# A hybrid decoder block: weights of the last two output jobs kept unsplit in scratch, and some loads moved to ScalarE's queue

## The chip, the core and the metric

The kernel runs on one core of a Trainium2 chip. The metric is device time in microseconds (us), the median of several runs. A profile of one further execution shows what each engine did: TensorE (PE, with its weight loads as PEld), VectorE (DVE), ScalarE (ACT), GpSimd (POOL) and SyncE (SP), which here issues most DMAs.

## The reference

One decoder block on a sequence of 2048 positions, width 1024, in float32. A normalised and modulated input is projected by `w_in` (1024 x 8192). One branch is a convolution, a gated linear recurrence and a product with `w_out_rnn`; the other is attention in three dilated windows and a product with `w_out_attn`. Both are merged by sigmoid gates and go through `w_o`:

```python
    y_rnn = (hr * jax.nn.silu(z_rnn.astype(jnp.float32))).astype(dt) @ w_out_rnn[l]
    ...
    y_attn = (o * jax.nn.silu(z_attn.astype(jnp.float32))).astype(dt) @ w_out_attn[l]
    merged = jax.nn.sigmoid(g_r + bg_r) * y_rnn + jax.nn.sigmoid(g_a + bg_a) * y_attn
    x = x + gate[:, None, :] * (merged @ w_o[l])
return rms_norm(x, g_final)
```

Each of `w_out_rnn`, `w_out_attn` and `w_o` is 1024 x 1024.

## The kernel before

**Split operands.** TensorE multiplies in float32r, a shortened float32. Each operand is therefore split into a high part, a copy made by ACT (`hi_act`, L157), and a low part, the operand less its high part, made by POOL (`lo_pool`, L163) or DVE (`lo_dve`, L166). A product is three matmuls (`mm3`, L149): high x high, high x low, low x high.

**Stage one, to about 1372 us.** The input projection is computed by a seven-product scheme (Strassen's) on 512-wide blocks: per product four steps of `mm3`. Its split operands go once to a scratch tensor `sD` and are loaded again, seven tiles ahead. Between these products, from 812 to 1282 us, `output_weights` prepares the two output projections: every five products it takes one of 32 pieces of 512 x 128, first the 16 of `w_out_rnn` (i = 0), then the 16 of `w_out_attn` (i = 1). It loads the piece into a tile `R` one product after its start, splits it after four (ACT, then POOL) and stores high and low part after six, from ACT's queue, into `wD[i, m, half]`. There each partition's high and low values lie side by side, 4 KB in a row.

**Stage two, to about 1960 us.** Attention, head by head. Between its pieces runs a generator, `steps`, that computes the two output projections as eight jobs: four blocks of 512 positions for the recurrence (weights i = 0, results into `mrT`), then four for attention (i = 1, results into `meT`). A job has eight tiles (m) of 128 output channels, a tile has eight steps (k), and a step is one `mm3` of 128 x 128 weights with 128 x 512 inputs `yh`, `yl`. Two weight tiles serve one output tile, four steps each:

- `load_w` at steps 1 and 5 issues, on SP, the load of the weight tile that is needed three half-tiles later (`load_wd`, L339, 512 KB from `wD`), into one of four buffers S0 to S3; it waits until TensorE is done with the buffer's last content.
- `load_g` at step 3 loads, on SP, this tile's gates and for attention also the recurrence's part: `fg<-gaT`, `fg<-mrT` (L1695, 256 KB each), from a pool of four buffers.
- `evict` at step 1 of the following tile multiplies PSUM by the gate (L1700, DVE) and adds the recurrence's part (L1702, DVE). There are two PSUM tiles.
- `store` at step 7 of the following tile stores the result from SP (L1707, `meT<-fg`).
- `load_y` and `split_y` fetch the next job's inputs (`R<-oT`, L345) and split them.

**Stage three, about 1960 to 2074 us.** The last 128 steps, which are the last two jobs (attention, blocks 2 and 3), run after attention has ended. A hand-written table fires further work after each step s = 0 to 127: `load_rows(k)` for k = 0 to 3 loads two 128 x 1024 pieces of `w_o` (L1827, on SP) at the start and at s = 16, 44 and 75; `build_rows(s, k)`, from s = 8, 32, 72 and 96, multiplies them by the gate (L1830, POOL, `gate_rows`) and forms sums and split parts B11 to T4 of the next stage (L1842 on DVE for the sums, then ACT with DVE or POOL); `load_left(0)` at s = 104 loads the first 1 MB of `meT` in two DMAs (L1879, SP).

**Stage four, to the end.** The product with `w_o`, again by seven products, the residual and the last normalisation.

Inside stages two and three the order on each engine is the order in which the code was written; buffers of a pool are assigned when the program is built. Every DMA of SP and ACT uses one of eight completion counters in turn, so it also waits for the DMA eight before it to have landed.

Of the kernel before, what the change touches and what calls it, by code (L numbers as in the profile page):

```python
# [10 lines left out]
F32 = mybir.dt.float32  # L11
F32R = mybir.dt.float32r
# [8 lines left out]
P = 128  # L21
S = 2048
D = 1024
KT = D // P
NB = 4
# [64 lines left out]
def decoder_block(ctx, tc, x, c, positions, g_norm, w_mod, b_mod, w_in, b_gate, conv_w, conv_b,  # L90
# [4 lines left out]
    def T(pool, shape, dt, tag, **kw):  # L95
        cnt[0] += 1
        return pool.tile(shape, dt, tag=tag, name=f"{tag}_{cnt[0]}", **kw)
# [3 lines left out]
    def scratch(name, shape):  # L101
        return nc.dram_tensor(name, shape, F32, kind="Internal").ap()
# [16 lines left out]
    sD = scratch("sD", [28 * 7, P, 2, KH, P])  # L119

    wD = scratch("wD", [2, KT, 2, P, 2, KH, P])

    cp = ctx.enter_context(tc.tile_pool(name="cp", bufs=1))
    class Pools:
# [31 lines left out]
    def hi_act(o, i):  # L156
        nc.scalar.activation(o, i, AF.Copy)  # L157
# [177 lines left out]
    def load_wd(i, m, half):  # L335
        x = n_w[0]
        n_w[0] += 1
        W[x] = t = T(pS, [P, 2, KH, P], F32R, f"S{x % 4}")
        nc.sync.dma_start(t[:].bitcast(F32), wD[i, m, half])  # L339
# [80 lines left out]
    def output_weights():  # L420

        parts = [(i, w, m, half) for i, w in enumerate((w_out_rnn, w_out_attn)) for m in range(KT) for half in range(2)]
        for x, (i, w, m, half) in enumerate(parts):
            v = {}

            def load(v=v, w=w, m=m, half=half):
                v["raw"] = raw_tile([P, KH, P])
                rows = slice(half * KH * P, (half + 1) * KH * P)
                nc.sync.dma_start(v["raw"][:], w[0, rows, m * P : (m + 1) * P].rearrange("(k p) m -> p k m", p=P))

            def split(v=v):
                v["h"] = T(wq, [P, KH, P], F32R, "s1", bufs=1)
                v["l"] = T(wq, [P, KH, P], F32R, "s2", bufs=1)
                hi_act(v["h"][:], v["raw"][:])
                lo_pool(v["l"][:], v["raw"][:], v["h"][:])

            def store(v=v, i=i, m=m, half=half):
                for l, n in enumerate("hl"):
                    nc.scalar.dma_start(wD[i, m, half, :, l], v[n][:].bitcast(F32))

            for d, fn in ((1, load), (4, split), (6, store)):
                after_prod.setdefault(n_prod[0] + 5 * x + d, []).append(fn)

    def total(dst, ps, u, perm=lambda ap: ap):
# [1202 lines left out]
            at(e + 2, TAIL, self.store)  # L1647

    stored = set()


    def steps(jobs):

        tiles = [(j, m) for j in range(len(jobs)) for m in range(KT)]
        Y, G = {}, {}

        def load_w(x):

            if x < 2 * len(tiles):
                assert x == n_w[0]  # L1660
                j, m = tiles[x // 2]
                load_wd(jobs[j][0], m, x % 2)

        def load_y(j, k):
            if j < len(jobs):
                w, ys, n = jobs[j]
                if ys is oT and (n, k) == (2, KT - 1):

                    Y0[False, n, k] = last_head[0].zt[:, 0].rearrange("p r j -> p (r j)")
                    return  # L1670
                if ys is oT and n == 2 and k >= KH:

                    t = T(ap_, [P, KQW], F32, "kraw", bufs=4)
                    nc.sync.dma_start(t[:, :CH], ys[k * P : (k + 1) * P, n * CH : (n + 1) * CH])
                    Y0[False, n, k] = t[:, :CH]
                    return
                assert ys is yaT or (n // 2, k, n % 2) in stored
                load_yd(ys, n, k)

        def split_y(j, k):  # L1680
            if j < len(jobs):
                Y[j, k] = yh, yl = [T(fl, [P, CH], F32R, tag, bufs=NY) for tag in ("yh", "yl")]
                w, ys, n = jobs[j]
                t = Y0.pop((ys is yaT, n, k))
                hi_act(yh[:], t[:])
                (lo_dve if k % 2 else lo_pool)(yl[:], t[:], yh[:])

        def load_g(t):
            j, m = tiles[t]
            w, ys, n = jobs[j]  # L1690
            at_ = slice(m * P, (m + 1) * P), slice(n * CH, (n + 1) * CH)
            G[t] = []
            for src in (grT,) if ys is yaT else (gaT, mrT):
                g = T(fl, [P, CH], F32, "fg", bufs=4)
                nc.sync.dma_start(g[:], src[at_])  # L1695
                G[t].append(g)

        def evict(t, ps):
            g = G[t]
            nc.vector.tensor_tensor(g[0][:], ps[:], g[0][:], ALU.mult)  # L1700
            if len(g) > 1:
                nc.vector.tensor_tensor(g[0][:], g[0][:], g[1][:], ALU.add)  # L1702

        def store(t):
            j, m = tiles[t]
            w, ys, n = jobs[j]
            nc.sync.dma_start((mrT if ys is yaT else meT)[m * P : (m + 1) * P, n * CH : (n + 1) * CH], G.pop(t)[0][:])  # L1707

        for k in range(KT):
            split_y(0, k)  # L1710
        yield
        last = None
        for t, (j, m) in enumerate(tiles):
            ps = T(pj, [P, CH], F32, "pj")
            for k in range(KT):
                if k % KH == 1:

                    load_w(2 * t + k // KH + 3)
                if k == 1 and t:
                    evict(t - 1, last)  # L1720
                if k == 3:
                    load_g(t)
                if k == 7 and t:
                    store(t - 1)
                wt = W[2 * t + k // KH]
                yh, yl = Y[j, k]
                mm3(ps[:], wt[:, 0, k % KH, :], wt[:, 1, k % KH, :], yh[:], yl[:], first=k == 0, last=k == KT - 1)
                if k % KH == KH - 1:
                    W.pop(2 * t + k // KH)


                x = m * KT + k - KT * (KT - 1)
                j1 = j + 1
                if m == 0:
                    x, j1 = x + KT * KT, j

                if j1 == NB + 2:

                    if -14 <= x < KT - 14:
                        load_y(j1, x + 14)  # L1740
                elif j1 and x in LOAD_Y:
                    load_y(j1, LOAD_Y[x])
                if j1 and x in SPLIT_Y:
                    split_y(j1, SPLIT_Y[x])
                yield
            last = ps
        evict(len(tiles) - 1, last)
        store(len(tiles) - 1)
# [75 lines left out]
    def load_rows(k):  # L1824
        for i in range(2):
            v[k, i] = t = stage(1 + i + 2 * (k % 2), [P, D])
            nc.sync.dma_start(t[:], w_o[0, (k + i * KH) * P : (k + i * KH + 1) * P, :])  # L1827

    def gate_rows(k, i):
        nc.gpsimd.tensor_tensor(v[k, i][:], v[k, i][:], v["gate"][:], ALU.mult)  # L1830
# [44 lines left out]
    def load_left(p):  # L1875
        for half in range(2):
            shape = [P, KH, 2 * P]
            A[p, half] = t = T(up[0], shape, F32, f"A{half}", bufs=2) if p else stage(1 + half, shape)
            nc.sync.dma_start(t[:], meT[half * KH * P : (half + 1) * KH * P, p * 2 * P : (p + 1) * 2 * P]  # L1879
                              .rearrange("(k p) j -> p k j", p=P))  # L1880

    def left(p, name):
# [161 lines left out]
    with tc.manual_schedule():  # L2044
        v["gate"] = stage(0, [P, D])
        nc.sync.dma_start(v["gate"][:], gateD[0:1, :].broadcast_to([P, D]))
        load_rows(0)
        for k in range(KH):
            build_rows((8, 32, 72, 96)[k], k)
            if k:  # L2050
                on((16, 44, 75)[k - 1], load_rows, k)
        on(LAST - 24, load_left, 0)
        early = {}
        for p in range(NP):
            for d, fn, args in left_events(p):
                x = 7 * p + d - 4
                if p or d > 2:
                    on_p(max(x, 1), fn, *args)
                else:
                    on(LAST - 12 + 4 * (d + 1), fn, *args)  # L2060
            if p:
                on_p(max(7 * p - 12, 0), load_left, p)
            if p > 1:
                on_p(7 * p - 2, load_rows_x, p)
        for s in range(LAST):
            next(fill)
            fire(s)
        next(fill, None)
        fire(LAST)
        assert not pend  # L2070
        pools.close("fl", "pR")
        up.append(pools.open("up", side="right", bufs=1))
        v["gf"] = T(up[0], [P, D], F32, "gf")
        load_rows_x(0)
        load_rows_x(1)
        nc.sync.dma_start(v["gf"][:], g_final.unsqueeze(0).broadcast_to([P, D]))
        fire_p()
        for p in range(NP):
            output_pair(p)
        assert not after  # L2080
# [30 lines left out]
```

## Time and profile before

| | us |
|---|---|
| median of 3 runs (2241.41 to 2246.01) | 2245.79 |
| the profiled execution | 2239.79 |
| its span, from first to last instruction | 2238.0 |

| engine | busy us | share of the span |
|---|---|---|
| PE | 2171.1 | 97% |
| PEld | 1834.1 | 82% |
| DVE | 1403.2 | 63% |
| ACT | 1267.8 | 57% |
| POOL | 1054.7 | 47% |

Over the whole span the DMA engines moved 580.99 MB, 260 GB/s. Matmuls overlap, so a busy share of PE is not its rate; the distance between the starts of matmuls is. In a row of the profile stand the source line, the engine, the operation, what it writes and reads, the count, the busy time and mean duration, and, after the bar, how long the engine was idle before it and what ended that.

### The profile page before, as it was taken

The page shows a single profiled execution, that of the slowest core. Times are in us where ns is not written, and L with a number is a line of the kernel's source. Part 1 is how long each engine was busy: PE and PEld are TensorE (multiplying, and loading weights), DVE is VectorE, ACT ScalarE, POOL GpSimd, SP SyncE. Part 2 cuts the span into 40 slices and gives each one's busy share as a digit, 9 for nine tenths or more (in the row PEclk, how much of TensorE's full clock was granted, in tenths as well). Part 3 has the DMA queues.
Part 4 walks back from the last instruction along what each step waited for, and adds up shares of the span by engine and source line. Part 5 has one row for each costly group of instructions (what it writes and reads, how often), then busy time and mean ns, then how long its engine had stood idle before and what let it go on. Part 6 is the DMA issues. An engine that isn't in the chain of part 4 may idle for free. (4 is left out here: it accounts for less than half of the span.)

```text
span 2238.0 us, 33996 instructions
## 1 busy us (share of the span) xinstructions
PE 2171.1 (97%) x11326; PEld 1834.1 (82%) x11326; DVE 1403.2 (63%) x2452; ACT 1267.8 (57%) x2524; POOL 1054.7 (47%) x784
## 2 busy tenths in 40 slices
PE   8999999999999999999999999999999998988998
PEld 5998888888778998888788887888888887866786
DVE  5838887878456815444445342566677777645787
ACT  6638678667543627556546302676778877522333
POOL 2457777767557422222222112455566666344443
PEclk9999999999999999999999999999999999999999
DMA  8367887887998368888888988987888886899543
GB/s 286 118 210 260 286 297 269 293 283 263 319 278 295 113 231 272 284 288 282 275 286 283 343 290 287 288 269 246 267 261 265 243 266 218 253 331 321 196 161 113
DMA packets 409827, 580.99 MB, mean 260 GB/s; under 512 B 72150, under 2 KB 270002, under 8 KB 408628
## 3 DMA queue, kind: packets, MB, share of 16 engines
q1 hardware_dynamic: 371668, 458.81, 64.5%
q10 hardware_dynamic: 37792, 119.97, 14.0%
q8 instruction: 90, 1.47, 0.3%
q14 instruction: 85, 0.70, 0.1%
q0 software_dynamic: 192, 0.05, 0.0%
HBM read 364.78 MB, written 213.91 MB: 259 GB/s over the span
## 5 line engine op out<-in xcount | busy, mean ns | idle before, releaser
L149 PE MATMUL pj<-yh,S 128*128 128x512 f32 x1024 | 372.3, 408 | 21.8 <-DMA S<-wD 10.6
L163 POOL TENSOR_TENSOR S<-R,S 128x512 fp32r<-128x512 f32 x168 | 256.0, 1532 | 173.1 <-ACT S L157 70.4
L149 PE MATMUL X<-T,S 128*128 128x512 f32 x1344 | 324.4, 390 | 4.4 <-ACT u L383 3.3
L149 PE MATMUL V<-T,S 128*128 128x512 f32 x1344 | 324.6, 390 | 3.6 <-DVE t L450 3.3
L149 PEld LDWEIGHTS X<-T,S 128*128 128x128 f32 x1344 | 251.3, 188 | 59.4 <-ACT u L383 5.0
L149 PEld LDWEIGHTS V<-T,S 128*128 128x128 f32 x1344 | 251.8, 188 | 58.3 <-DVE t L450 3.2
L149 PEld LDWEIGHTS pj<-yh,S 128*128 128x128 f32 x1024 | 195.6, 191 | 64.2 <-ACT yh L157 8.6
L149 PE MATMUL pj<-yl,S 128*128 128x512 f32 x512 | 204.5, 399 | 7.5 <-POOL yl L163 5.9
L163 POOL TENSOR_TENSOR S<-s,S 128x512 fp32r<-128x512 f32 x92 | 139.7, 1519 | 116.5 <-ACT S L157 73.0
L1417 ACT ACTIVATE pp<-pp,st 128x256 f32<-128x256 f32 (+3 forms) x256 | 133.8, 524 | 93.3 <-DVE st L1416 92.1
L149 PE MATMUL Z<-T,S 128*128 128x512 f32 x672 | 161.9, 390 | 0.0
L149 PE MATMUL Y<-T,S 128*128 128x512 f32 x672 | 161.8, 390 | 0.0
L149 PE MATMUL W<-T,S 128*128 128x512 f32 x672 | 161.6, 389 | 0.0
L149 PEld LDWEIGHTS W<-T,S 128*128 128x128 f32 x672 | 126.0, 188 | 27.0 <-issue 0.9
L149 PEld LDWEIGHTS Y<-T,S 128*128 128x128 f32 x672 | 125.9, 188 | 26.0
L149 PEld LDWEIGHTS Z<-T,S 128*128 128x128 f32 x672 | 125.8, 188 | 26.1
L166 DVE TENSOR_TENSOR ptl<-pT,pth 128x384 fp32r<-128x384 f32 (+1 forms) x160 | 97.8, 628 | 75.4 <-ACT pth L157 73.2
L163 POOL TENSOR_TENSOR s<-R,s 128x512 fp32r<-128x512 f32 x32 | 45.2, 1413 | 206.4 <-ACT s L157 189.2
L157 ACT ACTIVATE S<-R 128x512 fp32r<-128x512 f32 x168 | 101.5, 621 | 47.6 <-DMA R<-in_w_in_dram 21.8
L908 DVE SCALAR_TENSOR_TENSOR xc<-xr,par,xc 128x512 f32<-128x512 f32 x96 | 99.3, 1034 | 44.8 <-ACT xc L902 42.5
L1481 ACT ACTIVATE pp<-pp,M 128x256 f32<-128x256 f32 (+3 forms) x256 | 118.0, 523 | 10.0 <-DVE M L1604 10.0
L1416 DVE CUSTOM_DVE_ANT_0 pp<-sc,msk 128x256 f32<-128x256 f32 (+3 forms) x256 | 104.6, 448 | 24.0 <-PE sc L149 21.8
(398 smaller groups left out, 4786.0 us busy)
## 6 DMA issues: line engine op xcount, KB each, us to landing
sD<-S ACTq DMA_DIRECT2D x196, 512.0 KB, 4.0
S<-sD SPq DMA_DIRECT2D x196, 512.0 KB, 4.8
S<-wD SPq DMA_DIRECT2D x128, 512.0 KB, 5.7
R<-in_w_in_dram SPq DMA_DIRECT2D x136, 256.0 KB, 4.2
wD<-s ACTq DMA_DIRECT2D x64, 256.0 KB, 5.4
T<-in_w_mod_dram SPq DMA_DIRECT2D x8, 1024.0 KB, 11.8
vN<-ev SPq DMA_DIRECT2D x64, 128.0 KB, 2.7
zaT<-ev SPq DMA_DIRECT2D x32, 256.0 KB, 4.7
```

Of the source, the lines that this page charges most:

```text
L149: nc.tensor.matmul(o, lhsT=l, rhs=r, start=st, stop=sp, **kw)
L157: nc.scalar.activation(o, i, AF.Copy)
L163: nc.gpsimd.tensor_tensor(o, i, h.bitcast(F32), ALU.subtract)
L166: return nc.vector.tensor_tensor(o, i, h.bitcast(F32), ALU.subtract).ins
L908: nc.vector.scalar_tensor_tensor(xc, xr[:, i : i + CH], cw(i), xc, ALU.mult, ALU.add)
L1416: nc.vector.tensor_tensor_reduce(pdst, s_ps, mask, 1.0, 3e38, ALU.add, ALU.min, m_)
L1417: nc.scalar.activation(pdst, pdst, AF.Exp, bias=m_, scale=-1.0, accum_out=l_)
L1481: nc.scalar.activation(pp, pp, AF.Copy, scale=w)
```

## The change

A second scratch tensor `wR` holds the pieces of `w_out_attn` unsplit. In `output_weights` each of the 16 pieces with i = 1 is now also stored there as loaded, from ACT's queue, three products after its start; the split and both stores to `wD` stay.

In `steps`, weight tiles with an index over `RAW` = 97, which are the last 30 of 128, are no longer loaded from `wD`: a 256 KB load from `wR` (2 KB per partition) goes into the low half of the buffer. The new `split_w`, called at steps 0 and 4 of each tile for the weight tile of the following half-tile, makes the high part by ACT and then the low part in place by DVE.

`load_rows(k)` for k = 1 to 3 and `load_left(0)` are issued by ACT's queue and no longer by SP's. The builds start two steps later, at s = 10, 34, 74 and 98.

```diff
+    wR = scratch("wR", [KT, 2, P, KH, P])
...
-            for d, fn in ((1, load), (4, split), (6, store)):
+            def store_raw(v=v, m=m, half=half):
+                nc.scalar.dma_start(wR[m, half], v["raw"][:])
+
+            for d, fn in ((1, load), (3, store_raw), (4, split), (6, store)) if i else ((1, load), (4, split), (6, store)):
                 after_prod.setdefault(n_prod[0] + 5 * x + d, []).append(fn)
...
+    RAW = 2 * KT * (NB + 2) + 1
...
-                load_wd(jobs[j][0], m, x % 2)
+                if x <= RAW:
+                    load_wd(jobs[j][0], m, x % 2)
+                    return
+
+                n_w[0] += 1
+                W[x] = t = T(pS, [P, 2, KH, P], F32R, f"S{x % 4}")
+                nc.sync.dma_start(t[:, 1].bitcast(F32), wR[m, x % 2])
+
+        def split_w(x):
+            if RAW < x < 2 * len(tiles):
+                raw = W[x][:, 1].bitcast(F32)
+                hi_act(W[x][:, 0], raw)
+                lo_dve(W[x][:, 1], raw, W[x][:, 0])
...
             for k in range(KT):
+                if k % KH == 0:
+                    split_w(2 * t + k // KH + 1)
                 if k % KH == 1:
                     load_w(2 * t + k // KH + 3)
...
-            nc.sync.dma_start(t[:], w_o[0, (k + i * KH) * P : (k + i * KH + 1) * P, :])
+            (nc.scalar if k else nc.sync).dma_start(t[:], w_o[0, (k + i * KH) * P : (k + i * KH + 1) * P, :])
...
-            nc.sync.dma_start(t[:], meT[half * KH * P : (half + 1) * KH * P, p * 2 * P : (p + 1) * 2 * P]
+            (nc.sync if p else nc.scalar).dma_start(t[:], meT[half * KH * P : (half + 1) * KH * P, p * 2 * P : (p + 1) * 2 * P]
...
-            build_rows((8, 32, 72, 96)[k], k)
+            build_rows((10, 34, 74, 98)[k], k)
```

## The prediction

> **What bounds the kernel now.** I read the profile's page first, then the windows, the groups of lines, the waits and the timelines of the one stage that the change rebuilds.
>
> ```profile
> PE 2171.1 (97%) x11326; PEld 1834.1 (82%) x11326; DVE 1403.2 (63%) x2452; ACT 1267.8 (57%) x2524; POOL 1054.7 (47%) x784
> PE   8999999999999999999999999999999998988998
> DMA  8367887887998368888888988987888886899543
> ```
>
> TensorE is busy almost everywhere. In the strip of 40 slices (56 us each) it drops to eight tenths in slices 36 and 37, 1958 to 2070 us, where the DMA row stands at 9 and 9. There the last two jobs of the output projection run.
>
> ```profile
> 1957.00 0.62 PE L149 MATMUL pj<-yh,S 128*128 128x512 f32 x2
> 1960.40 0.62 PE L149 MATMUL pj<-yh,S 128*128 128x512 f32 x2
> 1960.62:2074.30 113.68, 96.49 (x386) 74.53 (x384) 57.78 (x74) 24.07 (x40) 45.35 (x26) 0.94 0.91 321
> 2012.41:2037.57 25.16, 22.39 (x73) 16.99 (x74) 9.72 (x12) 6.83 (x11) 11.76 (x7) 0.77 0.90 312
> 2037.57:2054.75 17.18, 16.48 (x73) 13.36 (x72) 11.19 (x14) 3.65 (x6) 8.19 (x4) 1.00 0.90 321
> L149 PE MATMUL pj<-yh,S 128*128 128x512 f32 x257 | 86.3, 409 | 15.8 <-DMA S<-wD 10.2 <-DVE s L1842 3.7 <-ACT yh L157 1.7
> ```
>
> The first two rows (TensorE's timeline) lie five steps of three matmuls apart: 3.40 / 5 = 0.68 us a step when nothing is missing, so 128 steps are 87.0 us. The windows give span, busy times of PE, PEld, DVE, ACT and POOL, granted clock, DMA share and GB/s: the 16 tiles took 113.68 us, that is 26.7 us more than 87.0, with the DMA engines busy for 0.91 of it. The matmuls' own row puts 10.2 us of idle time to the weight loads and 3.7 to a DVE instruction that is not theirs. The clock of 0.77 in the second window costs about 25.16 x 0.23 = 5.8 us; 5 of it I count as following from stalls. The third window shows that TensorE can run almost without gaps (16.48 of 17.18) in this stage.
>
> ```profile
> 1984.68 0.50 PE L149 MATMUL pj<-yh,S 128*128 128x512 f32 x1 [1.68 <-DMA S<-wD]
> 1988.51 0.32 SPq L1695 DMA_DIRECT2D fg<-mrT  x1
> 1988.92 0.38 SPq L339 DMA_DIRECT2D S<-wD  x1
> 1993.76 0.69 DVE L1702 TENSOR_TENSOR fg<-fg,fg 128x512 f32<-128x512 f32 x1 [2.73 <-DMA fg<-mrT]
> 1994.48 0.32 SPq L1695 DMA_DIRECT2D fg<-mrT  x1
> 1995.06 0.47 PE L149 MATMUL pj<-yh,S 128*128 128x512 f32 x1 [1.56 <-DVE s L1842]
> 2001.75 0.86 SPq L1827 DMA_DIRECT2D st<-in_w_o_dram  x2
> 2002.70 1.81 SPq L339 DMA_DIRECT2D S<-wD  x1
> 2012.41 0.77 PE L149 MATMUL pj<-yh,S 128*128 128x512 f32 x1 [5.20 <-DMA S<-wD]
> 2013.40 1.05 PE L149 MATMUL pj<-yh,S 128*128 128x512 f32 x2
> 2065.98 0.50 PE L149 MATMUL pj<-yh,S 128*128 128x512 f32 x1 [1.80 <-DMA S<-wD]
> SPq L1695 <- DMA fg<-mrT: 24.5, 11, 4.0
> DMA to landing us min/median/max: 5.6/7.2/8.9
> ```
>
> Two patterns make the losses. First a loop through one buffer: the built program gives every tile's `mrT` load the buffer of the tile before, so SP waits at L1695 until DVE's addition L1702 has read it, 1988.51 to 1994.48, 5.97 us a round against the 5.44 us (8 x 0.68) of a tile. The weight load behind it on SP, issued at 1988.92, lands no sooner than 5.6 us later (the last row, for L339 in this stage): the matmul starts at 1995.06. So the wait put down to `s` is a weight load's, and S costs 10.2 + 3.7 = 13.9 us. Second, weight loads queued behind large ones: the pair of `w_o` rows goes out at 2001.75, the weights at 2002.70, and TensorE stands 5.20 us, after which two matmuls take 1.05 us and not 0.62. The waits of 1.68 and 1.80 us stand behind the pair of k = 1 and the pair from `meT`.
>
> **The change, part by part.**
>
> *Half the bytes of 30 weight loads.*
>
> ```profile
> DMA packets 14900, 36.54 MB, mean 321 GB/s; under 512 B 1570, under 2 KB 2594, under 8 KB 14894
> q1 hardware_dynamic: 14894, 36.47, 91.0%
> S<-wD SPq DMA_DIRECT2D x29, 512.0 KB, 7.2
> fg<-mrT SPq DMA_DIRECT2D x16, 256.0 KB, 5.6
> st<-in_w_o_dram SPq DMA_DIRECT2D x7, 512.0 KB, 8.0
> ```
>
> These are the stage's DMA rows. 0.91 x 113.68 = 103.4 us of engine time for 36.54 MB is 2.83 us/MB. A raw load is 256 KB (0.262 MB) less, 0.74 us; 30 of them take 7.86 MB or 22.2 us out, which leaves 81.2 us, and 89 us at the same fill of 0.91. So after the change neither the DMA engines (89) nor TensorE (87.0) forces more than about 89 us: at most 113.7 - 89 = 24.7 us can be won here.
>
> *The split, 30 times.*
>
> ```profile
> L157 ACT ACTIVATE yh<-R 128x512 fp32r<-128x512 f32 x8 | 5.0, 630 | 18.7 <-DMA R<-oT 12.6 <-PE pj L149 6.2
> L1702 DVE TENSOR_TENSOR fg<-fg,fg 128x512 f32<-128x512 f32 x16 | 16.5, 1029 | 12.7 <-DMA fg<-mrT 12.5
> L1700 DVE TENSOR_TENSOR fg<-pj,fg 128x512 f32<-128x512 f32 x16 | 11.1, 691 | 40.7 <-DMA fg<-gaT 20.4 <-PE pj L149 14.0 <-issue 6.3
> L166 DVE TENSOR_TENSOR B11l<-st,B11h 128x512 fp32r<-128x512 f32 x4 | 2.7, 681 | 0.0
> L166 DVE TENSOR_TENSOR T2l<-s,T2h 128x512 fp32r<-128x512 f32 x4 | 7.1, 1783 | 0.0
> L163 POOL TENSOR_TENSOR T3l<-st,T3h 128x512 fp32r<-128x512 f32 x4 | 6.9, 1736 | 18.9 <-ACT T3h L157 18.9
> L1830 POOL TENSOR_TENSOR st<-st,st 128x1024 f32<-128x1024 f32 x8 | 20.2, 2549 | 6.8 <-DMA st<-in_w_o_dram 6.8
> ```
>
> Same shapes: 0.630 us on ACT, then 0.681 on DVE, with the hand-overs about 1.4 us between landing and matmul. An ordinary weight load lands 0.74 us sooner for its own size and 0.74 for that of the weights still ahead of it in the queue: 1.5 against 1.4, nothing either way. ACT has room: 24.07 + 30 x 0.63 = 43 us. DVE has less: 57.78 + 30 x 0.681 = 78.2. The row T2l is the same operation as B11l and takes 1.10 us more, in all four places beside POOL's T3l. POOL is busy for 45.35 of 113.68, so some 12 of 30 splits may meet it: 13 us more, DVE at 91. Queued behind a split that waits for its weights are the two evictions L1700 and L1702, and behind those SP's next `mrT` load and store. I charge 1.5 us of TensorE time; the bounds are 0 and the third rival.
> The Trainium skill (SBUF — State Buffer, "SBUF: two separate sides") says that DVE and GpSimd share one port pair under an exclusive lock, and that the loser is blocked for the whole instruction. The 1783 against 681 ns agree, and by that rule alone a split could stand for a whole L1830 of POOL (2549 ns).
>
> *The `w_o` rows of k = 1 to 3 and the first `meT` pair move to ACT's queue.* Eight issues leave SP (0.86 us for two) and stand on ACT between its splits. In the built program a DMA may start once the eighth before it, on whichever queue, has landed; an issue that waits so holds up the splits behind it on ACT. The longest such wait of SP here is 4.0 us; four pairs of that would cost 16 us, and I take nothing, since eight DMAs back are about a tile and a half, 8 us or more, against landings of 5.6 to 8.0. In the SP queue a weight load behind such a pair has 1.05 MB x 2.83 = 3.0 us ahead of it. From another queue, if the two interleave evenly, it meets only its own size, 0.74: 2.2 us saved. Of the four waits that make the 10.2 us, three are behind pairs that move (5.20, 1.68 and 1.80); the one behind k = 0 stays. Gain 2.2 + 1.68 + 1.80 = 5.7 us, between 0 and 8.7. The clock lost after the longest stall follows it in half: 2.5 us, between 0 and 5.
> No row here shows two queues loading at once in this stage: q1 has 91.0% and ACT's queue nothing.
> The Trainium skill speaks on both sides: DMA: Bandwidth & Descriptors, "Issuing engines are not separate DMA queues", says that a second issuing engine saves only sequencer time; "Queues, rings and completion order" says that an engine goes round robin over the rows that have work. By the first sentence the 5.7 + 2.5 us stay lost.
>
> *The loop through `mrT`.* With 0.74 us less ahead of it the round of 5.97 becomes 5.2, just under a tile's 5.44. Of the 3.7 us I count 2.5 won (0 to 3.7), since the new placement of the buffers gives five more tiles' `mrT` a buffer whose content is still being stored to `meT`. The eight `R` loads (ACT yh 1.7 us) gain with the queue: 1 us. The builds that start two steps later (10, 34, 74, 98) keep their distance to the last step: nothing.
>
> *Earlier: 16 raw stores.*
>
> ```profile
> 1040.00:1285.00 245.00, 242.91 (x1077) 200.11 (x1076) 112.07 (x146) 127.53 (x191) 56.76 (x43) 1.00 0.89 296
> ACT s L157 <- DMA R<-in_w_out_attn_dram: 8.6, 6, 3.2
> PE pg L1021 <- DVE ev L1016: 2.1, 1, 2.1
> ```
>
> In this stretch TensorE waits once, 2.1 us, and not for DMA. The stores add 16 x 0.262 = 4.2 MB to 296 GB/s x 245 us = 72.5 MB: DMA 0.89 to 0.94. ACT now waits for the raw tile a product earlier, up to 2.7 us each, with 117 us of it idle. Covered by the seven weight tiles loaded ahead; I take 0.5 us. If the cover went, 4.2 MB x 0.89 x 245 / 72.5 = 12.6 us.
>
> **The sum.** 5.7 + 2.5 + 2.5 + 1 = 11.7 won, 1.5 + 0.5 lost: about 10 us. The profiled execution took 2239.79 us (span 2238.0); it would take 2229.8. It lies 6 us under the median of the three runs, 2245.79, so I give 2235.8 against that. 0.2% (4.5 us) is about what a measurement of this kernel can tell from no change.
>
> **Rivals.**
> 1. *The queue makes no difference (no change).* Loads still meet on the same DMA engines and the split eats what the bytes give: of the 11.7 only 3.5 (loop and `R`) remain, less 2, so 1.5 us: 2244. For it: an ordinary load comes out at 1.5 against 1.4. Against: 22 us of engine time leave a stage at 0.91. Chance 0.18.
> 2. *The stage falls to its floor.* The loop goes under 5.44 for good, splits stay clear of POOL: 89 us, 24 less: 2222. For it: the window from 2037.57 on runs so already, at a DMA share of 0.90. Against: bursts of `w_o` and `R` remain. Chance 0.18.
> 3. *DVE becomes the bound (slower).* Splits meet POOL and stand like T2l: 57.78 + 30 x 1.783 = 111.3 us of DVE, in order with the evictions; a quarter of its present waits for DMA (12.5 + 20.4 us in the rows L1702 and L1700) on top, 8, gives 119: 5.6 us slower than 113.7, with 0.5 earlier about 2252. It decides once the splits average over 1.6 us: 57.78 + 48 + 8 is then the 113.7 of today. For it: all four T2l. Against: only T2l of the four low parts per row is that long. Chance 0.16.
> My forecast, 2230 to 2241, has 0.48.
>
> **How the numbers follow.** Faster by over 0.2%: 0.48 + 0.18 = 0.66; within: 0.18; slower: 0.16. The range leaves a tenth out on each side: 2223 (near the floor) to 2250 (most of rival 1, the edge of rival 3).
>
> **What would show it.** The stage from the first matmul of its 16 tiles to the last step: 102 us, under 95 for rival 2, 110 to 114 for rival 1, over 117 for rival 3. S loads land in about 5.5 us rather than 7.2. The wait of 5.20 us falls to about 3, and the granted clock rises above 0.94. The new DVE rows S<-S average 0.7 to 1.2 us; over 1.6 is rival 3. `fg<-mrT` lands in about 4.9. If 1040 to 1285 shows TensorE waiting for DMA S<-sD, the cover of the stores was gone and I am wrong there.

## The result and the profile after

The changed kernel takes 2251.98 us (median of 6 runs, 2251.15 to 2254.16) against 2243.53 us of the kernel before on the same chip (6 runs, 2241.41 to 2246.01). The ratio is 1.0038 with a 95% interval of 1.0025 to 1.0050: slower by 8.5 us, where the prediction had 10 us faster and a range that ended at 2250. The execution that was profiled took 2252.27 us (span 2250.5).

First the page of the changed kernel, as shown of before:

```profile
PE 2183.3 (97%) x11326; PEld 1843.5 (82%) x11326; DVE 1442.4 (64%) x2482; ACT 1282.9 (57%) x2554; POOL 1060.3 (47%) x784
PE   8999999999999999999999999999999998988998
DMA  8467887887998368888989989888988887877543
```

TensorE's strip is the same as before, but in slices 36 and 37 the DMA row has come down from 9 9 to 7 7. The windows (span; busy PE, PEld, DVE, ACT, POOL; granted clock, DMA share, GB/s) of the 16 tiles and of the earlier stretch with the raw stores:

```profile
1964.90:2087.11 122.21, 103.26 (x385) 77.82 (x384) 93.92 (x104) 40.14 (x69) 48.76 (x26) 0.89 0.74 235
1040.00:1285.00 245.00, 244.10 (x1083) 201.39 (x1082) 115.00 (x147) 128.10 (x193) 58.39 (x43) 1.00 0.94 313
```

The 16 tiles took 122.21 us, 8.5 more than 113.68. The DMA share fell from 0.91 to 0.74, so the relief for the DMA engines came, and TensorE is slower all the same. Of the 8.5 us only 1.8 are idle time (122.21 - 103.26 = 18.95 against 113.68 - 96.49 = 17.19). The other 6.8 are matmuls that run longer, at a clock of 0.89 and not 0.94. DVE is busy for 93.92 us, up from 57.78. (In the second window, TensorE is busy for 244.10 of 245 us beside the raw stores.) Now the groups of lines of this stage:

```profile
L150 PE MATMUL pj<-yh,S 128*128 128x512 f32 x257 | 89.9, 429 | 14.8 <-ACT S L158 9.0 <-DVE S L167 5.7
L167 DVE TENSOR_TENSOR S<-S 128x512 fp32r<-128x512 f32 x30 | 30.5, 1025 | 9.3 <-ACT S L158 9.3
L1849 POOL TENSOR_TENSOR st<-st,st 128x1024 f32<-128x1024 f32 x8 | 21.4, 2700 | 6.3 <-DMA st<-in_w_o_dram 6.3
L158 ACT ACTIVATE S<-S 128x512 fp32r<-128x512 f32 x30 | 18.4, 626 | 47.8 <-DMA S<-wR 22.3 <-PE pj L150 12.1 <-DVE fg L1719 6.4
L1717 DVE TENSOR_TENSOR fg<-pj,fg 128x512 f32<-128x512 f32 x16 | 11.0, 684 | 15.9 <-PE pj L150 12.8 <-DMA fg<-gaT 3.0
L1861 DVE TENSOR_TENSOR st<-st,s 128x512 f32<-128x512 f32 x4 | 7.0, 1760 | 0.0
```

(Line numbers grew: L1717 and L1719 are the two evictions, L1849 the gate multiplication, L1861 the differences of the builds.) Before, TensorE's idle time stood at the weight loads (10.2 us). None of it does now; in its place stand the high part by ACT (9.0) and the low part by DVE (5.7). The DMA rows of the stage:

```profile
DMA packets 14919, 28.71 MB, mean 235 GB/s; under 512 B 1577, under 2 KB 2601, under 8 KB 14912
q10 hardware_dynamic: 1920, 4.19, 10.2%
S<-wR SPq DMA_DIRECT2D x29, 256.0 KB, 4.4
fg<-mrT SPq DMA_DIRECT2D x16, 256.0 KB, 4.4
```

The bytes fell from 36.54 to 28.71 MB, by 7.83 where the prediction had 7.86. Weights land in 4.4 us, not 7.2. The worst place, by the timelines of GpSimd, DVE, ACT and TensorE:

```profile
1990.77 1.72 POOL L164 TENSOR_TENSOR T3l<-st,T3h 128x512 fp32r<-128x512 f32 x1
1992.44 5.58 POOL L1849 TENSOR_TENSOR st<-st,st 128x1024 f32<-128x1024 f32 x2
...
1991.29 1.74 DVE L167 TENSOR_TENSOR S<-S 128x512 fp32r<-128x512 f32 x1
1992.95 0.68 DVE L1717 TENSOR_TENSOR fg<-pj,fg 128x512 f32<-128x512 f32 x1
1993.66 2.16 DVE L1719 TENSOR_TENSOR fg<-fg,fg 128x512 f32<-128x512 f32 x1
1995.75 2.82 DVE L1861 TENSOR_TENSOR st<-st,s 128x512 f32<-128x512 f32 x1
...
1998.61 0.63 ACT L158 ACTIVATE T4h<-st 128x512 fp32r<-128x512 f32 x1 [8.27 <-DVE st L1861]
1999.14 1.13 ACT L158 ACTIVATE S<-S 128x512 fp32r<-128x512 f32 x2
...
1993.08 0.73 PE L150 MATMUL pj<-yh,S 128*128 128x512 f32 x2 [2.64 <-DVE S L167]
1999.81 0.80 PE L150 MATMUL pj<-yh,S 128*128 128x512 f32 x1 [4.16 <-ACT S L158]
```

And the window that begins there:

```profile
1999.81:2005.00 5.19, 5.19 (x12) 4.09 (x13) 4.37 (x7) 2.25 (x4) 0.00 (x0) 0.50 0.57 203
```

Beside GpSimd's T3l a split takes 1.74 us on DVE, and TensorE stands 2.64. Beside the two gate multiplications an eviction takes 2.16 and a difference 2.82, against 0.68 for the same work alone. ACT waits 8.27 us for that difference with two splits queued behind it, and TensorE stands 4.16. What comes after stands in the window: twelve matmuls in 5.19 us, 0.43 each and not 0.227 (a third of the step of 0.68), at a granted clock of 0.50. A split is called four steps before the first matmul that needs it, 4 x 0.68 = 2.7 us; that is all the slack there is for its two halves and for what stands ahead of them on ACT and DVE.

### The profile page after: what moved, and what is told of

It reads as the page before. It is cut to its first block, busy times and chain, and to the rows that moved or that the text cites. A ratio compares the mean times of both kernels' runs of the same rounds, so it can differ in the third digit from the quotient of the medians.

```text
span 2250.5 us, 34124 instructions
## 1 busy us (share of the span) xinstructions
PE 2183.3 (97%) x11326; PEld 1843.5 (82%) x11326; DVE 1442.4 (64%) x2482; ACT 1282.9 (57%) x2554; POOL 1060.3 (47%) x784
## 4 chain that ended last, share of the span: by engine, by line
PE 52%; DMA 7%; DVE 4%; issue 4%; ACT 3%; POOL 3%; SPq 1%; ACTq 0%; POOLq 0%; DVEq 0%
PE X L150 10%; PE pj L150 10%; PE V L150 9%; PE W L150 5%; PE Z L150 5%; PE Y L150 4%; PE sc L150 4%; PE o L150 3%; DMA R<-in_w_in_dram 1%; PE pg L150 1%; PE pT L1505 1%; PE pT L1518 1%; DMA vraw<-vN 1%; DMA kraw<-qT 1%; DMA kraw<-kT 1%
## 5 line engine op out<-in xcount | busy, mean ns | idle before, releaser
L150 PEld LDWEIGHTS pj<-yh,S 128*128 128x128 f32 x1024 | 197.9, 194 | 65.7 <-ACT S L158 11.5
L150 PE MATMUL pj<-yl,S 128*128 128x512 f32 x512 | 206.9, 404 | 10.3 <-POOL yl L164 5.6
L150 PEld LDWEIGHTS pj<-yl,S 128*128 128x128 f32 x512 | 99.7, 195 | 29.4 <-POOL yl L164 7.7
## 6 DMA issues: line engine op xcount, KB each, us to landing
T<-in_w_mod_dram SPq DMA_DIRECT2D x8, 1024.0 KB, 11.7
```

What stands on the lines that cost most here:

```text
L150: nc.tensor.matmul(o, lhsT=l, rhs=r, start=st, stop=sp, **kw)
```

## The experiments

Theory: the smaller loads bring what was forecast, but the splits stand in order on ACT and DVE between the builds; GpSimd stretches DVE's work, the splits come late, TensorE stops and then runs at half clock. Rivals: the moved issues, the raw stores, or the sheer volume of DVE's work. Every ratio is against the kernel before on the same chip; "us" is the ratio less one, times 2243. The stage is the span of the 16 tiles in the profiled execution. There is one such execution of each kernel, and it can lie up to 5 us from the median (2236.52 against 2241.68 for the moved issues alone). So the ratios decide, and the stages only show where the time is.

| kernel | median us | ratio (95%) | us | stage us |
|---|---|---|---|---|
| the change | 2251.98 | 1.0038 (1.0025 to 1.0050) | +8.5 | 122.21 |
| moved issues alone | 2241.68 | 0.9987 (0.9977 to 0.9997) | -2.9 | 108.89 |
| raw loads and splits alone | 2250.54 | 1.0029 (1.0019 to 1.0039) | +6.5 | 119.84 |
| raw stores alone | 2244.02 | 0.9999 (0.9989 to 1.0009) | -0.2 | 114.78 |
| change, no gate on GpSimd | 2240.48 | 0.9979 (0.9968 to 0.9989) | -4.7 | 111.90 |
| change, T4 later | 2249.66 | 1.0031 (1.0018 to 1.0044) | +7.0 | 119.26 |
| change, no split | 2229.55 | 0.9937 (0.9925 to 0.9950) | -14.1 | 103.13 |
| change, high part only | 2237.50 | 0.9977 (0.9966 to 0.9989) | -5.2 | 108.46 |
| change, ten raw loads | 2242.08 | 0.9988 (0.9977 to 1.0000) | -2.7 | 111.01 |
| change, GpSimd's work on DVE | 2232.69 | 0.9954 (0.9936 to 0.9972) | -10.3 | 102.77 |
| change, gate in halves | 2246.14 | 1.0011 (1.0000 to 1.0023) | +2.5 | 116.58 |
| moved issues, gate in halves | 2239.92 | 0.9987 (0.9977 to 0.9997) | -2.9 | 111.48 |
| change, low part on GpSimd | 2245.17 | 1.0008 (0.9998 to 1.0018) | +1.8 | 118.29 |
| moved issues, GpSimd's work on DVE | 2239.13 | 0.9986 (0.9976 to 0.9996) | -3.1 | 110.12 |
| change, GpSimd's work on DVE, T4 later | 2234.73 | 0.9966 (0.9952 to 0.9979) | -7.6 | 103.99 |

**The parts of the change, each alone.** The moved issues with the later builds:

```diff
-            nc.sync.dma_start(t[:], w_o[0, ...])
+            (nc.scalar if k else nc.sync).dma_start(t[:], w_o[0, ...])
...
-            nc.sync.dma_start(t[:], meT[...])
+            (nc.sync if p else nc.scalar).dma_start(t[:], meT[...])
...
-            build_rows((8, 32, 72, 96)[k], k)
+            build_rows((10, 34, 74, 98)[k], k)
```

> The kernel before with the eight issues (w_o rows of k = 1 to 3, first meT pair) on ACT's queue and the builds two steps later; no raw loads, no splits, no raw stores. Theory (the splits, queued on ACT and DVE between the builds, make the loss; the move of the issues is harmless): no slower than before, 2236 to 2244 us, stage of 16 tiles 106 to 113 us, and no wait of TensorE over 4 us for a weight load. Rival (issues that wait on ACT's queue, and the later builds, make the loss): slower than before by 4 us or more, stage 118 us or more, with ACT standing at its own DMA issues. The prediction's own term for the move was 5.7 + 2.5 us won, 2236.

The changed kernel with these put back, the `meT` pair too:

```diff
-            (nc.scalar if k else nc.sync).dma_start(...)
+            nc.sync.dma_start(...)
...
-            build_rows((10, 34, 74, 98)[k], k)
+            build_rows((8, 32, 72, 96)[k], k)
```

> The changed kernel with the eight issues back on SP and the builds back at steps 8, 32, 72 and 96: raw stores, raw loads and splits alone. Theory (splits in line behind the builds' waits for DVE, which GpSimd slows): about as slow as the changed kernel, 2249 to 2256 us, stage 118 us or more, TensorE again standing 3 us or more for the high and low parts S at the tiles in which a row is gated on GpSimd. Rival (the moved issues): back to 2236 to 2244 us, stage under 113 us. If both this and the kernel with the moved issues alone come out faster than before, the two parts only hurt together.

The raw stores alone: the changed kernel with the issues and the builds put back as above, and with no weight tile read from `wR`:

```diff
-    RAW = 2 * KT * (NB + 2) + 1
+    RAW = 2 * KT * 2 * NB
```

> The kernel before with the 16 raw stores alone (nothing is loaded from them). Theory: they cost under 1 us, 2243 to 2245 us. Rival (they cost the 4 us by which the changed kernel was behind before tile 48 of the output projection): 2247 us, with the drift again between tiles 0 and 48. The prediction charged 0.5 us, and 12.6 us if the loads ahead gave no cover.

The windows of the three, each in a fence of its own. The moved issues, with ACT's DMA queue and TensorE's waits for weights (total, times, longest) behind:

```profile
1961.86:2070.75 108.89, 94.43 (x386) 72.28 (x384) 63.32 (x74) 23.34 (x39) 45.50 (x26) 0.97 0.96 335
```

```profile
q10 hardware_dynamic: 1920, 4.19, 9.9%
```

```profile
PE pj L149 <- DMA S<-wD: 7.5, 7, 2.1
```

The raw loads and splits alone, then the raw stores alone:

```profile
1964.51:2084.35 119.84, 99.87 (x385) 76.12 (x384) 94.45 (x104) 40.25 (x69) 49.42 (x26) 0.91 0.74 242
```

```profile
1961.50:2076.28 114.78, 96.85 (x385) 74.81 (x384) 56.79 (x74) 25.67 (x43) 46.16 (x27) 0.94 0.92 321
```

All three came out as the theory had it. The loads on ACT's queue take the wait of 5.20 us away: the longest is 2.1, and the kernel is 2.9 us faster. The raw stores cost nothing. The raw loads with their splits alone are the loss. (The 4 us by which the changed kernel was behind at the first of the 16 tiles, counted from the first tile of the output projection, need not come from the change: that stretch took 588.3 to 592.7 us in the profiled executions, 592.1 in one without any raw tile and 589.4 in one with all of them.)

**How much each half of the split costs.** Three kernels leave part of the computation out, so that what is left can be timed. Without the split TensorE reads the raw weights twice:

```diff
-                if k % KH == 0:
-                    split_w(2 * t + k // KH + 1)
...
-                mm3(ps[:], wt[:, 0, k % KH, :], wt[:, 1, k % KH, :], ...
+                hi = 0 if 2 * t + k // KH <= RAW else 1
+                mm3(ps[:], wt[:, hi, k % KH, :], wt[:, 1, k % KH, :], ...
```

> The changed kernel without any split: TensorE reads the raw weights for the high and the low part alike, so the split of the 30 weight tiles is left out of the computation. It shows what the smaller loads alone are worth. Theory (the smaller loads gain what the prediction said or more, the splits eat more than that): stage 92 to 102 us, 2224 to 2234 us. Rival (the stage is held by the loads' latency or by the builds, the bytes are worth little): stage 105 us or more, 2237 us or more.

With the high part only:

```diff
                 hi_act(W[x][:, 0], raw)
-                lo_dve(W[x][:, 1], raw, W[x][:, 0])
```

> The changed kernel with the high part of each split on ACT and without the low part on DVE: TensorE reads the raw weights as the low part, so the 30 subtractions are left out. Theory B (DVE is the engine that makes splits late): close to the kernel without any split, 2226 to 2237 us, stage 95 to 105 us. Theory A (ACT's order makes them late): still 2243 us or more, stage 113 us or more, ACT waiting for T4's difference with the high parts S behind it.

Without the gate on GpSimd:

```diff
-        on(s, gate_rows, k, 0)
-        on(s + 5, gate_rows, k, 1)
```

> The changed kernel without the multiplication of the w_o rows by the gate on GpSimd (eight instructions of 2.7 us); that part of the computation is left out. Theory (GpSimd beside DVE stretches the builds' differences and the splits, and the splits behind them come late): DVE's difference st<-st,s falls from 1.76 to under 1.3 us, the waits of 8.3 us and 5.1 us of ACT for it go, TensorE's waits of 4.55 and 3.1 us at the fifth and thirteenth tile shrink below 2 us, stage 104 to 112 us, 2232 to 2243 us. Rival (the in-order place of the splits alone, or DVE's sheer load, makes the loss): stage 118 us or more, time within 4 us of the changed kernel.

The three windows, in the order of the text, and TensorE's row of the last:

```profile
1961.46:2064.59 103.13, 93.70 (x385) 73.27 (x384) 64.48 (x74) 23.24 (x39) 44.84 (x26) 0.97 0.86 276
```

```profile
1962.15:2070.61 108.46, 96.31 (x386) 74.39 (x385) 68.48 (x74) 39.36 (x70) 48.12 (x26) 0.95 0.82 267
```

```profile
1964.58:2076.48 111.90, 99.57 (x386) 74.88 (x384) 81.36 (x104) 39.36 (x69) 27.66 (x18) 0.94 0.79 258
```

```profile
L150 PE MATMUL pj<-yh,S 128*128 128x512 f32 x257 | 87.1, 416 | 10.3 <-DVE S L167 5.2 <-ACT S L158 4.2 <-ACT yh L158 0.8
```

The smaller loads and the moved issues bring 14.1 us as long as nothing is split (11.2 more than the moved issues alone). Each step after that is worked out from the ratios: the high parts on ACT take back 14.1 - 5.2 = 8.9 us, the low parts on DVE another 5.2 + 8.5 = 13.7. Both halves matter. That the high part alone costs so much was not expected: 2237.50 us and 108.46 lie between the ranges of theory B (2226 to 2237, 95 to 105) and theory A (2243 or more, 113 or more). There TensorE waits 7.3 us for high parts, and ACT 15.1 us for T4's difference, which still takes 1.78 us on DVE; that this makes the 8.9 us is not shown, since the high part alone was not tried with a quiet GpSimd. Without the gate multiplication the change is 4.7 us faster than before: those eight GpSimd instructions cost it 13.2 us. There the difference L1861 is back at 684 ns, as expected, but ACT's waits for it stayed at 15.0 us in all, and TensorE still stood 2.24 and 2.56 us for the low part at two places, in the first and the last build. At both a split of 1.74 to 1.75 us on DVE stands behind two instructions of 1.77 to 1.79, beside GpSimd's low parts B22, T1 and T3. So the gate is not the only work of GpSimd that makes splits late.

**Order on ACT, or DVE itself?**

```diff
-        on(s + 17, high, "T4", k)
+        on(s + 20, high, "T4", k)
...
-        on(s + 18, low, "T4", k, lo_dve)
+        on(s + 21, low, "T4", k, lo_dve)
```

> The changed kernel with ACT's high part T4 (and DVE's low part of it) three steps later, so that it no longer stands ahead of the split of the weights. Theory A (order on ACT: the split waits behind T4, which waits for DVE): TensorE's waits at the fifth and thirteenth tile (4.55 and 3.1 + 1.8 us) and the half clock after them go, stage 112 to 117 us, 2242 to 2247 us. Theory B (DVE itself is late, since GpSimd holds it; ACT's order only shows it): the low part S is late instead, stage 119 us or more, 2249 us or more.

The timelines of DVE, ACT and TensorE:

```profile
1996.94 2.86 DVE L1861 TENSOR_TENSOR st<-st,s 128x512 f32<-128x512 f32 x1
1999.83 0.63 ACT L158 ACTIVATE T4h<-st 128x512 fp32r<-128x512 f32 x1 [7.59 <-DVE st L1861]
...
2001.05 0.90 PE L150 MATMUL pj<-yh,S 128*128 128x512 f32 x2 [2.16 <-DVE S L167]
```

Theory B: 7.0 us slower than before. At the place shown above, the split that TensorE needs next no longer waits behind T4 for its high part (the split after it still does), but DVE is in the same gate-stretched chain (2.86 us), and TensorE waits for the low part.

**Single stalls, or the volume of DVE's work?** The changed kernel with everything that GpSimd does beside the splits given to DVE:

```diff
-        nc.gpsimd.tensor_tensor(v[k, i][:], v[k, i][:], v["gate"][:], ALU.mult)
+        nc.vector.tensor_tensor(v[k, i][:], v[k, i][:], v["gate"][:], ALU.mult)
...
-        on(s + 14, low, "B22", k, lo_pool)
+        on(s + 14, low, "B22", k, lo_dve)
...
-        on(s + 17, low, "T1", k, lo_pool)
+        on(s + 17, low, "T1", k, lo_dve)
...
-        on(s + 19, low, "T3", k, lo_pool)
+        on(s + 19, low, "T3", k, lo_dve)
...
-                (lo_dve if k % 2 else lo_pool)(yl[:], t[:], yh[:])
+                (lo_dve if k % 2 or j == 2 * NB - 1 else lo_pool)(yl[:], t[:], yh[:])
```

> The changed kernel with GpSimd's work beside the splits moved to DVE: the eight multiplications of the w_o rows by the gate, the low parts B22, T1 and T3 of the builds and the low parts of R. Nothing is left out. DVE then does about 74 x 0.68 for the kernel before, 30 x 0.68 for the splits, 16 x 0.68 for the low parts and 8 x 1.36 for the gate, about 92 us against the 93.9 us that it is busy in the changed kernel. Theory L (single long stalls of DVE while GpSimd runs make the splits late): the split S<-S falls from 1.025 to about 0.7 us, TensorE's waits shrink, 2240 to 2246 us, stage 109 to 116 us. Theory V (the volume of work on DVE, 92 to 94 us in order, makes them late however it comes about): same as the changed kernel, 2249 to 2256 us, stage 119 us or more.

The window, and three groups:

```profile
1962.41:2065.18 102.77, 93.96 (x386) 71.84 (x384) 83.80 (x128) 39.58 (x69) 1.55 (x2) 0.98 0.85 280
```

```profile
L167 DVE TENSOR_TENSOR S<-S 128x512 fp32r<-128x512 f32 x30 | 20.6, 688 | 10.7 <-ACT S L158 10.5
L1849 DVE TENSOR_TENSOR st<-st,st 128x1024 f32<-128x1024 f32 x8 | 9.7, 1218 | 0.0
L150 PE MATMUL pj<-yh,S 128*128 128x512 f32 x257 | 83.2, 401 | 8.0 <-ACT S L158 6.2 <-ACT yh L158 1.7
```

This is the fastest kernel here that computes all of the reference: 10.3 us faster than before. DVE runs 24 more instructions than in the changed kernel and is busy for 10 us less. All 30 splits take 0.68 to 0.69 us. In TensorE's row the waits for the low part S are gone (5.7 us in the changed kernel), those for the high part are 6.2 us (9.0). It came out better than theory L expected (2240 to 2246, a stage of 109 to 116), and volume is ruled out. Whether GpSimd's absence helps by itself is told by the kernel before with the moved issues and the same edit:

> The kernel before with the moved issues, ordinary weight loads (no splits, no raw stores), and GpSimd's gate and low parts on DVE. Theory (the smaller loads win as soon as their splits are not held up): only a little faster than the moved issues alone, 2237 to 2242 us, stage 105 to 111 us, with TensorE still waiting for DMA S<-wD. Rival (GpSimd's absence is the whole gain, the raw loads still bring nothing): 2230 to 2235 us, as fast as the changed kernel with everything on DVE (0.9954 of before).

Its window:

```profile
1961.37:2071.49 110.12, 97.30 (x386) 75.04 (x384) 64.04 (x95) 22.96 (x38) 1.08 (x1) 0.94 0.93 327
```

It does not: 0.9986 against 0.9987. Four kernels, two by two:

| us against before | GpSimd busy | its work on DVE |
|---|---|---|
| moved issues, ordinary loads | -2.9 | -3.1 |
| moved issues, raw loads and splits | +8.5 | -10.3 |

So with GpSimd busy the raw loads and splits lose 8.5 + 2.9 = 11.4 us; with GpSimd quiet they win 10.3 - 3.1 = 7.2. The loss needs both, the splits and GpSimd at work beside them.

The gate in halves leaves the work on GpSimd and only shortens its instructions:

```diff
-        nc.gpsimd.tensor_tensor(v[k, i][:], v[k, i][:], v["gate"][:], ALU.mult)
+        for j in range(2):
+            c = slice(j * CH, (j + 1) * CH)
+            nc.gpsimd.tensor_tensor(v[k, i][:, c], v[k, i][:, c], v["gate"][:, c], ALU.mult)
```

> The changed kernel with each multiplication by the gate cut into two of half the columns on GpSimd (16 instructions of about 1.35 us for 8 of 2.7). Theory L (DVE stands for as long as one GpSimd instruction lasts): DVE's longest split and subtraction, 2.85 us now, fall to about 2 us, and with gaps between the halves DVE goes ahead: 2245 to 2250 us. Rival (DVE gets nowhere in the gaps, the sum of GpSimd's work counts): same as the changed kernel, 2250 to 2254 us, and splits of 2.8 us are still there.

The window, the group of the low parts, and the timelines of DVE and GpSimd at the place shown above:

```profile
1965.01:2081.59 116.58, 98.97 (x385) 73.75 (x384) 93.27 (x104) 39.82 (x69) 53.35 (x34) 0.94 0.76 246
```

```profile
L167 DVE TENSOR_TENSOR S<-S 128x512 fp32r<-128x512 f32 x30 | 31.7, 1066 | 10.8 <-ACT S L158 10.8
```

```profile
1993.85 1.77 DVE L1863 TENSOR_TENSOR st<-st,s 128x512 f32<-128x512 f32 x1
1995.54 1.75 DVE L167 TENSOR_TENSOR T2l<-s,T2h 128x512 fp32r<-128x512 f32 x1
1997.22 1.75 DVE L167 TENSOR_TENSOR S<-S 128x512 fp32r<-128x512 f32 x1
...
1991.64 6.78 POOL L1851 TENSOR_TENSOR st<-st,st 128x512 f32<-128x512 f32 x4
```

The average split is no shorter (1.066 us for 1.025) and DVE is as busy (93.27 for 93.92), yet 6 us are won. What changed is the longest split, 1.79 us in place of 2.85, and at the place shown the longest difference, 1.77 in place of 2.82. The timeline shows why they are shorter: GpSimd's four halves take 6.78 / 4 = 1.70 us each, and DVE gets one instruction through for each of them.

**Three smaller trials.** The same halves without any raw loads:

> The kernel before with the moved issues alone (0.9987 of before) and the gate cut into halves on GpSimd. Theory L: DVE's evictions wait less, mrT's load goes out sooner: 2238 to 2242 us. Rival: no difference from the moved issues alone, 2240 to 2243 us.

By the ratio no difference from the moved issues alone (0.9987 both), though the median of 2239.92 us lies in theory L's range; the two ranges were too close for intervals of 2.2 us each way. Shorter stalls of DVE bring 6.0 us where its splits feed TensorE, and nothing that could be measured where there are none.

The low part of the splits on GpSimd:

```diff
-                lo_dve(W[x][:, 1], raw, W[x][:, 0])
+                lo_pool(W[x][:, 1], raw, W[x][:, 0])
```

> The changed kernel with the low part of the 30 splits on GpSimd instead of DVE. DVE is relieved of about 30 us, GpSimd takes some 30 x 1.3 us more and the low parts stand in its order behind gate multiplications of 2.7 us and low parts of 1.7 us. If DVE's order and volume are all that matters: 2238 to 2246 us. If every operation of GpSimd also holds DVE, and its own order makes splits late (theory L): 2252 us or more.

The window, and the group of the low parts:

```profile
1962.13:2080.42 118.29, 99.62 (x385) 74.41 (x384) 81.44 (x74) 40.93 (x69) 91.37 (x56) 0.94 0.75 245
```

```profile
L164 POOL TENSOR_TENSOR S<-S 128x512 fp32r<-128x512 f32 x30 | 44.1, 1477 | 22.6 <-ACT S L158 22.4 <-POOL S L164 0.2
```

Theory L expected 2252 or more, and it is 2245: a miss. GpSimd is now the busier of the two, 91.37 us against DVE's 81.44, but no low part takes more than 1.75 us (1.27 at least), and 6.7 us come back. It lies in the range given for "DVE's order and volume" (2238 to 2246). The kernel with GpSimd's work on DVE rules out volume alone, but not order: here DVE's evictions and differences stand neither ahead of the low parts nor behind them. So this run does not tell whether the shorter maximum (1.75 us at an average of 1.48, against 2.85 at 1.025) or the shorter line brought the 6.7 us.

Ten raw loads, those that step numbers placed between the builds:

```diff
-    RAW = 2 * KT * (NB + 2) + 1
+    RAW = {2 * KT * (NB + 2) + x for x in (9, 10, 14, 15, 16, 17, 18, 19, 30, 31)}
...
-                if x <= RAW:
+                if x not in RAW:
...
-            if RAW < x < 2 * len(tiles):
+            if x in RAW:
```

> The changed kernel with raw loads for only ten of the weight tiles, those whose splits fall between the builds (6th and 7th half, 10 in all: two ahead of the second build, six around the change of job with its R loads, the last two), and ordinary loads for the others. Theory: the loads are smaller where R queues, and no split stands beside GpSimd: faster than the kernel with the moved issues alone (0.9987 of before), 2235 to 2241 us, stage 103 to 108 us. Rival (any split costs as much as its load saves): 2241 to 2245 us.

The group of the low parts:

```profile
L167 DVE TENSOR_TENSOR S<-S 128x512 fp32r<-128x512 f32 x10 | 12.6, 1260 | 3.2 <-ACT S L158 3.0
```

A miss: as fast as the moved issues alone, and in the rival's range. The choice by steps did not avoid GpSimd: five of the ten splits stood beside B22l, T3l, the low parts of R or a gate multiplication (1.34 to 2.85 us). So this run decides nothing between the two.

Last, T4 later where GpSimd is quiet:

> The changed kernel with GpSimd's work on DVE, and T4's high and low part three steps later. ACT waits 11.5 us for T4's difference without this, with high parts S queued behind. Theory A at this place: the waits of TensorE for the high part (6.2 us) shrink, 2227 to 2232 us. Rival (the difference is as late for the later place): no change, 2231 to 2235 us.

TensorE's row:

```profile
L150 PE MATMUL pj<-yh,S 128*128 128x512 f32 x257 | 83.7, 405 | 7.9 <-DVE S L167 3.0 <-ACT yh L158 2.9 <-ACT S L158 1.9
```

No gain (0.9966 against 0.9954; the intervals overlap). ACT's wait for T4's difference fell from 11.5 to 3.3 us and TensorE's for the high part from 6.2 to 1.9, but 3.0 us stood for the low part instead and 2.9 for the inputs (1.7 without the move): 7.9 us of idle time where there were 8.0.

## Why the prediction was wrong, point by point

The step that failed is the split: "1.5 against 1.4, nothing either way", and the charge of 1.5 us of TensorE time. In the changed kernel the 30 splits cost 14.1 + 8.5 = 22.6 us. With GpSimd's work on DVE the splits and that work together cost 14.1 - 10.3 = 3.8 us, give or take 4.9 by the two intervals, and the 1.5 us lies within that. So it was not the split's own work that was mis-sized but the lateness of splits in line beside GpSimd.

- **Half the bytes, the queue, the loop and R.** Forecast 11.7 us; 14.1 without splits, and a stage of 103.13 us where 102 was expected (102.77 with the splits and a quiet GpSimd). The totals agree in part by luck. Of the 11.7 the moved issues were to bring 8.2, and alone they brought 2.9; the loop and `R` were to bring 3.5. The other 11.2 of the 14.1 came with the smaller loads, whose earlier landing the prediction had set off against the split. Weights and `mrT` land sooner than forecast (4.4 us each; 5.5 and 4.9 expected).
- **The split in the abstract.** 0.626 us on ACT was right. On DVE the average of 1.025 us lies inside the 0.7 to 1.2 that the forecast named, and DVE's 93.92 us are near the forecast 78 to 91: eight splits met GpSimd where twelve were reckoned with. So the counts of work were about right and the conclusion was not. The prediction compared an average hand-over with an average saving at the landing. Yet a split waits in line, 22 of the 30 took at most 0.69 us and eight took 1.35 to 2.85, two of them (2.61 and 2.85) as long as a gate multiplication, the 2549 ns that the prediction named and did not price. At the place shown one of the eight stops TensorE for 2.64 us, and a stretched eviction and difference (2.16 + 2.82 us) stand ahead of the next two. The sum was made in busy time where it had to be made along the chain from landing to matmul.
- **The queue, 5.7 + 2.5 us.** Alone it gives 2.9 us (0.7 to 5.2 by its interval): the sign was right and the size about a third. The wait of 5.20 us did fall, to 2.1 at most, and the clock rose to 0.97. With GpSimd's work on DVE and ordinary loads the longest such wait was 2.2, at a clock of 0.94 all the same. The Trainium skill (DMA: Bandwidth & Descriptors, "Issuing engines are not separate DMA queues") grants a second issuing engine no more than sequencer time; the shorter waits, 2.1 and 2.2 us, speak for more here, though the builds moved with it and were not tried apart.
- **The moved issues do not add up with the raw loads.** -2.9 and +6.5 make +3.6 alone, and +8.5 together, a difference of 4.9 us. The half-widths of the three intervals are 2.2, 2.2 and 2.8 us, together about 4.2 (root of the sum of squares), so this may be little more than measurement. Whether the queue or the later builds would make it was not tried.
- **Raw stores, 0.5 us.** Right: 0.9999. The DMA share in 1040 to 1285 rose from 0.89 to 0.94 as worked out, and TensorE was busy for 244.10 of 245.
- **The loop through `mrT`.** In SP's waits (total, times, longest) stands:

```profile
SPq L1712 <- DMA meT<-fg: 10.0, 5, 3.2
```

SP now waits five times for a store to `meT`; the prediction counted five such tiles. No run shows that it costs TensorE anything.

- **The rivals.** The third gave the right time, 2252, by a mechanism that is half right: splits that meet GpSimd. The time owes something to luck, too: it stands on 2245.79, and as a loss it is 6.1 us, not 8.5. Its point of decision was wrong. It asked for an average over 1.6 us, so that DVE would be full; 1.025 was enough, with DVE busy for 77% of the stage. Full or not was not the question, as the kernel shows that has GpSimd's work on DVE. Its row T2l, 1.10 us longer in all four places, was the warning, and it was priced by how many splits it meets, not by who waits behind it. The row L1702 shown with it was a second one: 1029 ns on average and 2.33 us at most for an addition that takes 0.69 alone. So evictions, too, met GpSimd even before the change.
- **The clock.** It was expected over 0.94 and fell to 0.89. Matmuls that run longer are 6.8 of the 8.5 us, while TensorE's idle time grew by 1.8. Why nearly the same idle time cost more clock here was not tried apart; at the place shown stalls of 2.64 and 4.16 us follow each other within 10 us.

## What to carry to other kernels

Before work is put between a load's landing and the matmul, draw the chain at the worst place, with every instruction ahead of it on its engine at the duration it has beside GpSimd: averages and busy shares say little where the slack is a microsecond or two. If an in-order DVE feeds TensorE directly, look first at what GpSimd runs beside it; here moving GpSimd's work onto the "fuller" DVE turned a loss of 8.5 us into a gain of 10.3. Where GpSimd's work can't move, shorter instructions can help, since DVE waits for one of them at a time; here halves brought 6.0 us. A longer lead, a split called eight steps before its use and not four, was not tried.

## What the runs showed of the hardware

- In these timelines DVE and GpSimd take turns, one instruction for one, where DVE reads two operands from SBUF. Beside two gate multiplications of 2.79 us, DVE's difference took 2.82; beside halves of 1.70, its instructions took 1.75 to 1.77; alone, 0.68. The Trainium skill (SBUF — State Buffer, "SBUF: two separate sides") has the loser blocked for the whole instruction, and names among DVE's operations those with two SBUF inputs; the traces agree in both. The eviction L1717, with one input from PSUM, never took more than 0.695 us in its 64 instances in each of the 16 profiled kernels, while L1719, with both inputs in SBUF, took 2.16 at the place shown, right behind an L1717 of 0.68 beside the same gate multiplication. GpSimd's instructions are longer there as well: its low part T3l takes 1.72 us, and 1.30 in the kernel with the moved issues alone.
- The same gate multiplication takes 2.70 us on GpSimd in the changed kernel and 1.218 on DVE, so that taking it over costs DVE less time than one instruction loses beside it (2.82 - 0.68 = 2.14 us).
- After a stall of 4.16 us twelve matmuls ran at 0.43 us each, at a granted clock of 0.50. Against the kernel before, slower matmuls are 6.8 of the stage's 8.5 us. Against the kernel with GpSimd's work on DVE they are 9.3 of 19.4, and idle time 10.1.
